# Two-layer hybrid encoder: adds of squares on GpSimd, an earlier root, and border work of the MLP in another order

## The chip, the core and the metric

The kernel runs on one core of a Trainium2 chip. The metric is the device time of one execution in microseconds. Six actors matter: TensorE (PE, with its weight loads PEld), VectorE (DVE), ScalarE (ACT), GpSimd (POOL), SyncE (SP), which issues most loads, and the DMA engines. Each engine works through its own queue in a fixed order.

## The reference

A batch of one with 512 tokens of 1024 features goes through two residual layers and a final RMS norm, in float32. Layer 0 mixes tokens with two groups of attention heads, layer 1 with neighbourhood attention. Behind each stands the part that this change is about:

```
h = h + sq_relu_mlp(rmsnorm(h, norm_ffn[layer]), ffn_w_up[layer], ffn_w_down[layer])

def rmsnorm(x, g):
    y = x * rsqrt(mean(x * x, axis=-1) + EPS)
    return y * g

def sq_relu_mlp(h, w_up, w_down):          # 1024 -> 4096 -> 1024
    u = relu(h @ w_up)
    return (u * u) @ w_down
```

## The kernel before

**Layout.** The residual stream lies transposed in SBUF: `hT` has eight tiles of 128 features by 512 tokens. Every float32 product is made from rounded parts: a weight is split into a high and a low half (`whi` on ACT, L233 or L363; `wlo` on DVE, L223 or L364), an input likewise, and high x high, high x low and low x high are added in PSUM. So one product step is three matmuls of 512 columns (L606 to L608), and each step needs a `wlo` that DVE has made in time.

**A norm at a seam.** The factor of the RMS norm is put in late. For each feature tile k `split_g` makes the two halves of hT times the gain (L612 on ACT, L613 on DVE), and `sumsq_acc` squares the tile on ACT (L620) and adds the square to `acc` (L622). The sum of the first tile is its square itself, so there are seven adds, all on DVE. Then `compact_r` sums over the partitions by matmuls with a column of ones (L627), a root is made by a dozen small DVE operations (L629, L180 to L190), and transposes (L635) and an ACT copy spread it over all partitions as `rb`. There are three such seams: before the MLP of layer 0 (about 240 to 267 us), before the neighbourhood layer (about 579 to 605) and before the MLP of layer 1 (about 804 to 828). In the MLPs the whole root stands in `norm`, called before step 11 (layer 0) or 13 (layer 1) of the 32 steps of the first product `four`. At the neighbourhood seam `rows_r1` stands in the loop over the first value product.

**Seven products instead of eight.** The larger part of both MLP matrices goes through `Seven`: blocks of two by two weight tiles and two token halves, with sums of weight tiles made ahead (`seven_chunk`, L357 to L359) and seven products of 256 columns per pair of input tiles (L450 to L452). The weight sums are on GpSimd; in the four seven-products of the down matrix the fourth pair (kp == 3) has them on DVE. Results are put together on DVE (L459 to L462), and added to hT (L1576).

**The MLP in order.** The up matrix makes 32 tiles: six by plain steps (`plain`), the rest in pairs by seven-products; some of these pairs stay raw (`R`), and in layer 0 one pair more (`V`). The down matrix takes the first six tiles by `product`, the next eight by `product8` (eight banks of PSUM), then the raw pairs by four seven-products m = 0 to 3 (`u7`), and the last pair by plain steps (`gens4`). While `product8` runs, `convert` turns the raw pairs into what `u7` needs: differences on DVE (L391, L394, L423), then rounding on ACT (L418) and the low half on DVE (L419). It is a generator that `mlp` advances by a set pace per step of `product8`; beside it bias rows for the neighbourhood layer are written through SP (L1492, L1497). The plain pair of layer 0 is split (L966 on ACT, L963 on DVE) beside m = 0, after four of its steps.

**What sets the order.** Around attention the order is written out by hand (`fixed_order`). In the MLPs a planner of the framework places each engine's instructions by its own estimate of their times, within the dependences; what is wrapped in `keep_in_program_order` keeps its place. So a source edit at one place can move instructions at others.

Of the kernel before, what the change touches and what calls it, by code (L numbers as in the profile page):

```python
# [35 lines left out]
def encoder_kernel(ctx: ExitStack, tc: tile.TileContext, ins, out, dbg=None):  # L36
    nc = tc.nc
    PE, ACT, DVE, POOL, SP = nc.tensor, nc.scalar, nc.vector, nc.gpsimd, nc.sync
# [37 lines left out]
    def bank(tag, bufs):  # L76
        return ps.tile([P, 512], F32, tag=tag, bufs=bufs, name=nm(tag))

    def mmb():
        return bank("mm", 3)  # L80

    def sbk():
        return bank("s", 2)

    def stb():
        return bank("t", 2)

    def ob():
        return bank("o", 1)

    def scratch(dt=F32):
        return scp.tile([P, 512], dt, tag="sc", name=nm("sc"))
# [177 lines left out]
    def plan(*spec, make=None):  # L270
        asked.append((make or chunk, spec))
        return len(asked) - 1
# [96 lines left out]
    class Seven:  # L369
# [62 lines left out]

        def plan(self, w, c0, pairs=None):

            return [plan(w, pairs[kp] if pairs else 2 * kp, c0, DVE if pairs and kp == 3 else None, make=seven_chunk)
                    for kp in range(self.np)]

        def run(self, ids, evac):
# [130 lines left out]
    def tiles(c0, n):  # L569
        return [(c0 + o, min(P, n - o)) for o in range(0, n, P)]  # L570
# [46 lines left out]
    def sumsq_acc(k, acc, eng=None):  # L617

        sq = acc if k == 0 else scratch()
        ACT.activation(sq, hT[:, k, :], AF.Square)  # L620
        if k:
            (eng or POOL).tensor_tensor(acc, acc, sq, op=ALU.add)  # L622

    def compact_r(acc):
        b = stb()
        for i in range(4):
            PE.matmul(b[:, i : i + 1], acc[:, i * P : (i + 1) * P], ones[:, 0:1], start=True, stop=True)  # L627
        v = tiny(4)
        DVE.tensor_scalar(v, b[:, 0:4], 1.0 / D, EPS, op0=ALU.mult, op1=ALU.add)  # L629
        return rsqrt(v, 4)  # L630
# [8 lines left out]
    acc = pp.tile([P, S], F32, tag="p", name=nm("acc"))  # L639
# [701 lines left out]
    def first_product(l):  # L1341

        w = ins["ffn_w_up"][l]
        X = [Slot() for _ in range(KD)]
        acc = pp.tile([P, S], F32, tag="p", name=nm("acc"))
        for k in range(KD):
            split_g(hT[:, k, :], gffn(l, k), X[k].pair())
            sumsq_acc(k, acc, DVE)
        xp = [s_.pair() for s_ in X]
        U, R = [], []  # L1350
        rb = keep([P, S], F32, "rb")
# [10 lines left out]

        def norm():
            r = compact_r(acc)
            bk = stb()
            bcast_cols(lambda i: r[:, i : i + 1].to_broadcast([P, P]), P, bk)
            ACT.activation(rb, bk, AF.Copy)

        def x_sums(kp):
            raw = Slot(F32)  # L1370
# [39 lines left out]
        def plain():  # L1410
            four = product(w, 0, xp, tiles(0, 512), ev, lambda n: [mmb(), mmb(), mmb(), sbk()])
            two = product(w, 0, xp, tiles(512, 256), ev, lambda n: [sbk(), ob()], kstep=4)
            for n, _ in enumerate(four):
                if n == (11 if l == 0 else 13):
                    norm()
                if n == 14:
                    x_sums(0)
                    x_sums(1)
            for n, _ in enumerate(two):
                if n == 4:  # L1420
                    x_sums(2)
                if n == 6:
                    x_sums(3)
            flip[0] = 1
            for s_ in X:
                s_.free()
            state["plain"] = True
# [74 lines left out]
    def convert(u7, R):  # L1502
        held = tc.keep_in_program_order
        for kp, raw in enumerate(R):
            yield from u7.sums(kp, raw, DVE, held)
            yield
            yield from u7.split(kp, held)

    def mlp(l, last=None):

        stage, ahead, later = first_product(l)
        reserve[0] = 3
        w = ins["ffn_w_down"][l]
        up4, gens4 = [], []

        def plain_last(k0, V):
            left = list(V)  # L1520
            gens4.extend(product(w, k0, up4, tiles(512 * c, 512), lambda j, b, c=c: ev(4 * c + j, b), nk=2 * len(V))
                         for c in range(2))

            def beside(m, i):
                if m == 0 and i % 8 == 4 and left:
                    w_ = left.pop(0)
                    for z in range(2):
                        U4.append(Slot())
                        up4.append(U4[-1].pair())
                        split(w_.t[:, S * z : S * z + S], up4[-1])  # L1530
                    w_.free()

            return beside

        U4 = []

        def ev(m, b):
            return DVE.tensor_tensor(hT[:, m, :], hT[:, m, :], b, op=ALU.add)

        U, _, _, (at_u, _), _ = stage(SIZES[l][0])  # L1540
        up = [s_.pair() for s_ in U]
        gens = [product(w, at_u, up, tiles(512 * c, 512), lambda j, b, c=c: ev(4 * c + j, b)) for c in range(2)]
        ahead()
        for c, gen in enumerate(gens):
            for i, _ in enumerate(gen):
                later(c, i)
        for s_ in U:
            s_.free()
        U, R, V, (at_u, at_r), late = stage(*SIZES[l][1:])
        first = [k + z for k in at_u for z in range(2)]  # L1550
        gen = product8(w, first, U, ev)
        u7 = Seven(2 * len(R))
        ids = [u7.plan(w, 256 * m, at_r) for m in range(4)]
        k0 = 32 - 2 * len(V)
        beside = (last or plain_last)(k0, V)
        bias = iter(()) if last else bias_rows()
        reserve[0] = NSLOT
        work, at = convert(u7, R), 0
        for i, _ in enumerate(gen):
            if i in (1, 4, 6):  # L1560
                next(late, None)
            next(bias, None)

            at += 9 * len(R) + 2
            while at > 0:
                next(work, None)
                at -= 8 * len(U) - 2
        for x in (work, bias):
            for _ in x:
                pass  # L1570
        reserve[0] = 3
        for m in range(4):

            def evac(w_):
                h2 = hT[:, 2 * m : 2 * m + 2, :]
                DVE.tensor_tensor(h2, h2, w_.t.rearrange("p (z n) -> p z n", z=2), op=ALU.add)  # L1576

            for i, _ in enumerate(u7.run(ids[m], evac)):
                beside(m, i)
        u7.free()  # L1580
        if not last:
            hold["tables"].free()
        for gen in gens4:
            for _ in gen:
                pass
        for s_ in U4:
            s_.free()
# [5 lines left out]
    acc = pp.tile([P, S], F32, tag="p", name=nm("acc"))  # L1593
# [227 lines left out]
    for n, _ in enumerate(first):  # L1821
        if n == 2:
            for k in range(KD):
                sumsq_acc(k, acc, DVE)
        if n == 23:
            rows_r1()
    for _ in second:
# [247 lines left out]
```

## Time and profile before

| | us |
|---|---|
| median of 3 runs | 1160.41 (1160.13 to 1161.12) |
| profiled execution | 1159.82 |
| its span, first to last instruction | 1158.0 |
| mean granted TensorE clock | 0.998 |

A row of the timeline gives start and duration in us from the start of the span, engine, line, operation, tiles (written <- read), shape, and in brackets the idle time of the engine just before and what ended it; `x3` merges neighbours of one form. A matmul's duration is its passage through a pipeline, so the distance between two starts, not the duration, tells the rate. In a row of groups stand the busy time, the mean in ns of one, and the idle time before it. A row of a line's view has the shortest, the median and the longest duration in ns.

### The profile page before, as it was taken

How to read it: one execution, taken by the hardware profiler on the slowest of the kernel's cores; microseconds unless marked ns; L12 is line 12 of the kernel's file. 1: busy time of each engine (PE TensorE's matmuls, PEld its weight loads, DVE VectorE, ACT ScalarE, POOL GpSimd, SP SyncE). 2: the span in 40 equal slices, each digit the busy share in tenths (PEclk: the TensorE clock that was granted, in tenths of full speed). 3: DMA queues.
4: the chain of work that ended last, by engine and by line, in shares of the span. 5: the costliest groups of instructions: out<-in, count | busy, mean ns of one | idle time of the engine just before them, and what ended most of it. 6: DMA issues, size and time to landing. Idle time of an engine off the chain costs nothing.

```text
span 1158.0 us, 20534 instructions
## 1 busy us (share of the span) xinstructions
PE 1145.2 (99%) x7348; PEld 1022.7 (88%) x7348; DVE 893.7 (77%) x1568; ACT 669.2 (58%) x1135; POOL 585.3 (51%) x719
## 2 busy tenths in 40 slices
PE   9999999999999999999999999999999999999997
PEld 7787888888899999899988998988889999989995
DVE  7887988878867786977784666667997777688865
ACT  6676877755346668643453555555552666773445
POOL 4356252207688892369602232221388889435840
PEclk9999999999999999999999999999999999999999
DMA  7322415222523237823536574433344223381332
GB/s 236 104 73 72 99 55 137 65 67 96 172 76 98 86 92 192 217 88 110 159 98 164 142 181 119 127 107 119 100 155 127 74 85 99 74 200 58 126 119 73
DMA packets 115350, 134.37 MB, mean 116 GB/s; under 512 B 9795, under 2 KB 96752, under 8 KB 115248
## 3 DMA queue, kind: packets, MB, share of 16 engines
q1 hardware_dynamic: 110896, 120.09, 34.8%
q0 software_dynamic: 4032, 12.60, 5.4%
q8 instruction: 58, 0.95, 0.3%
q14 instruction: 44, 0.36, 0.1%
q10 hardware_dynamic: 320, 0.36, 0.1%
HBM read 110.61 MB, written 6.29 MB: 101 GB/s over the span
## 4 chain that ended last, share of the span: by engine, by line
PE 89%; DVE 5%; DMA 3%; ACT 1%; issue 1%; POOL 0%; SPq 0%; DVEq 0%; POOLq 0%; ACTq 0%
PE mm L606 8%; PE mm L607 8%; PE mm L608 8%; PE mm L452 4%; PE mm L450 4%; PE mm L451 4%; PE s L1130 3%; PE t L450 3%; PE t L452 3%; PE t L451 3%; PE o L1118 3%; PE s L452 2%; PE s L450 2%; PE s L451 2%; PE t L1105 2%; PE s L606 2%
## 5 line engine op out<-in xcount | busy, mean ns | idle before, releaser
L606 PE MATMUL mm<-a,whi 128*128 128x512 f32 x428 | 173.9, 407 | 0.2
L364 DVE TENSOR_TENSOR wlo<-a,whi 128x896 fp32r<-128x896 f32 x103 | 125.4, 1219 | 59.1 <-ACT whi L363 58.6
L608 PE MATMUL mm<-a,wlo 128*128 128x512 f32 x428 | 168.9, 396 | 0.0
L607 PE MATMUL mm<-a,whi 128*128 128x512 f32 x428 | 168.9, 395 | 0.0
L363 ACT ACTIVATE whi<-a 128x896 fp32r<-128x896 f32 x103 | 97.8, 950 | 111.4 <-PE s L451 27.4
L233 ACT ACTIVATE whi<-raw 128x1024 fp32r<-128x1024 f32 (+3 forms) x100 | 92.2, 924 | 68.4 <-PE s L607 24.3
L223 DVE TENSOR_TENSOR wlo<-raw,whi 128x1024 fp32r<-128x1024 f32 (+4 forms) x97 | 110.4, 1143 | 26.9 <-ACT whi L233 26.4
L452 PE MATMUL mm<-a,wlo 128*128 128x256 f32 x430 | 120.6, 280 | 0.4 <-DVE wlo L364 0.4
L450 PE MATMUL mm<-a,whi 128*128 128x256 f32 x430 | 120.8, 281 | 0.0
L451 PE MATMUL mm<-a,whi 128*128 128x256 f32 x430 | 120.5, 280 | 0.0
L363 ACT ACTIVATE whi<-raw 128x896 fp32r<-128x896 f32 x61 | 57.8, 952 | 80.2 <-POOL raw L359 36.1
L358 POOL TENSOR_TENSOR a<-a 128x256 f32<-128x256 f32 x103 | 97.8, 950 | 8.1
L364 DVE TENSOR_TENSOR wlo<-raw,whi 128x896 fp32r<-128x896 f32 x61 | 73.6, 1221 | 35.0 <-ACT whi L363 35.0
L359 POOL TENSOR_TENSOR a<-a 128x128 f32<-128x128 f32 x103 | 95.7, 929 | 8.1
L608 PEld LDWEIGHTS mm<-a,wlo 128*128 128x128 f32 x428 | 80.4, 188 | 18.2
L606 PEld LDWEIGHTS mm<-a,whi 128*128 128x128 f32 x428 | 80.5, 188 | 17.1 <-issue 0.9
L607 PEld LDWEIGHTS mm<-a,whi 128*128 128x128 f32 x428 | 80.7, 189 | 14.9 <-DVE a L963 0.2
L1718 POOL TENSOR_SCALAR p<-p,ti 128x256 f32<-128x256 f32 x64 | 35.8, 570 | 105.7 <-DVE ti L1717 90.7
L1138 POOL TENSOR_SCALAR p<-p,ti 128x512 f32<-128x512 f32 x64 | 45.3, 708 | 85.9 <-DVE ti L1137 59.9
L450 PE MATMUL t<-a,whi 128*128 128x256 f32 x312 | 87.6, 281 | 0.0
L451 PE MATMUL t<-a,whi 128*128 128x256 f32 x312 | 87.4, 280 | 0.0
L452 PE MATMUL t<-a,wlo 128*128 128x256 f32 x312 | 87.4, 280 | 0.0
(432 smaller groups left out, 3574.9 us busy)
## 6 DMA issues: line engine op xcount, KB each, us to landing
a<-in_ffn_w_up_dram SPq DMA_DIRECT2D x102, 256.0 KB, 2.8
raw<-in_ffn_w_down_dram SPq DMA_DIRECT2D x34, 512.0 KB, 4.1
raw<-in_ffn_w_down_dram SPq DMA_DIRECT2D x59, 256.0 KB, 2.7
raw<-in_od_w_qkv_dram SPq DMA_DIRECT2D x64, 128.0 KB, 3.3
raw<-in_ffn_w_up_dram SPq DMA_DIRECT2D x12, 512.0 KB, 3.9
wlo<-in_ffn_w_down_dram POOLq DMA_DIRECT2D x12, 512.0 KB, 7.0
a<-a SPq DMA_DIRECT2D x18, 256.0 KB, 3.2
bx<-a SPq DMA_DIRECT2D x32, 128.0 KB, 5.9
```

The source lines that it names most:

```text
L223: z = lambda: (eng or DVE).tensor_tensor(to, src, f32(high), op=ALU.subtract)
L233: ACT.activation(hi[:, 0:m], raw[:, 0:m], AF.Copy)
L358: held(eng.tensor_tensor(r[:, 4:6], r[:, 2:3].to_broadcast([P, 2, P]), r[:, 0:7:6], op=ALU.add))
L359: held(eng.tensor_tensor(r[:, 7], r[:, 3], r[:, 5], op=ALU.subtract))
L363: ACT.activation(hi[:, 0:896], raw[:, 128:1024], AF.Copy)
L364: DVE.tensor_tensor(lo[:, 0:896], raw[:, 128:1024], f32(hi[:, 0:896]), op=ALU.subtract)
L450: PE.matmul(o, wh, x[:, 0], start=kp == 0 and n in (0, 1, 3, 5), stop=False, skip_group_check=True)
L451: PE.matmul(o, wh, x[:, 1], start=False, stop=False, skip_group_check=True)
L452: PE.matmul(o, wl, x[:, 0], start=False, stop=kp == self.np - 1, skip_group_check=True)
L606: PE.matmul(o, wh, xh, start=first, stop=False)
L607: PE.matmul(o, wh, xl, start=False, stop=False)
L608: PE.matmul(o, wl, xh, start=False, stop=last)
```

## The change

Five edits. (1) At the three seams the adds of tiles 1 to 4 are made by GpSimd, those of tiles 5 to 7 by DVE. (2) `norm` is a generator with two parts, column sums with the root, and the spreading; they are called before steps 8 and 12 of `four` in layer 0, before steps 11 and 14 in layer 1. (3) In the first of the four seven-products of the down matrix (m = 0) the fourth pair's weight sums are on GpSimd too. (4) The plain pair of layer 0 is split beside m = 1. (5) `convert` is advanced by ten steps before `product8` begins, with the same pace afterwards, in both layers.

In the order in which the instructions of the two built programs stand, the following moves on TensorE: column sums (L627) and spreading (L635) stand 9 and 4 instructions earlier at the first seam; 20 and 17 earlier at the second; at the third the sums stand 4 later, because four low products that the planner had put behind them now stand in their places, and the spreading 4 earlier. On DVE one weight split (L223) moves out of the root's chain at the second seam, and one moves into it at the first; one of the plain pair's low halves (L963) moves behind the first evacuation of `u7`. On ACT the conversion's copies (L418) stand further ahead. On SP several loads of the down matrix (L252, L352) stand ahead of bias rows that they followed. Nothing else is added or removed: the matmuls, and the DMAs with their sizes, are the same.

```diff
--- before.py
+++ after.py
@@ -432,7 +432,8 @@
 
         def plan(self, w, c0, pairs=None):
 
-            return [plan(w, pairs[kp] if pairs else 2 * kp, c0, DVE if pairs and kp == 3 else None, make=seven_chunk)
+            return [plan(w, pairs[kp] if pairs else 2 * kp, c0, DVE if pairs and c0 and kp == 3 else None,
+                         make=seven_chunk)
                     for kp in range(self.np)]
 
         def run(self, ids, evac):
@@ -1345,7 +1346,7 @@
         acc = pp.tile([P, S], F32, tag="p", name=nm("acc"))
         for k in range(KD):
             split_g(hT[:, k, :], gffn(l, k), X[k].pair())
-            sumsq_acc(k, acc, DVE)
+            sumsq_acc(k, acc, DVE if k > 4 else POOL)
         xp = [s_.pair() for s_ in X]
         U, R = [], []
         rb = keep([P, S], F32, "rb")
@@ -1362,9 +1363,11 @@
 
         def norm():
             r = compact_r(acc)
+            yield
             bk = stb()
             bcast_cols(lambda i: r[:, i : i + 1].to_broadcast([P, P]), P, bk)
             ACT.activation(rb, bk, AF.Copy)
+            yield
 
         def x_sums(kp):
             raw = Slot(F32)
@@ -1410,9 +1413,10 @@
         def plain():
             four = product(w, 0, xp, tiles(0, 512), ev, lambda n: [mmb(), mmb(), mmb(), sbk()])
             two = product(w, 0, xp, tiles(512, 256), ev, lambda n: [sbk(), ob()], kstep=4)
+            factor = norm()
             for n, _ in enumerate(four):
-                if n == (11 if l == 0 else 13):
-                    norm()
+                if n in ((8, 12), (11, 14))[l]:
+                    next(factor)
                 if n == 14:
                     x_sums(0)
                     x_sums(1)
@@ -1522,7 +1526,7 @@
                          for c in range(2))
 
             def beside(m, i):
-                if m == 0 and i % 8 == 4 and left:
+                if m == 1 and i % 8 == 4 and left:
                     w_ = left.pop(0)
                     for z in range(2):
                         U4.append(Slot())
@@ -1556,6 +1560,8 @@
         bias = iter(()) if last else bias_rows()
         reserve[0] = NSLOT
         work, at = convert(u7, R), 0
+        for _ in range(10):
+            next(work)
         for i, _ in enumerate(gen):
             if i in (1, 4, 6):
                 next(late, None)
@@ -1821,7 +1827,7 @@
     for n, _ in enumerate(first):
         if n == 2:
             for k in range(KD):
-                sumsq_acc(k, acc, DVE)
+                sumsq_acc(k, acc, DVE if k > 4 else POOL)
         if n == 23:
             rows_r1()
     for _ in second:
```

## The prediction

> **What bounds the kernel now.** I read the page's busy shares and chain first, then every start of a matrix product in the timeline, and then the queues that stand behind the few late starts.
>
> ```profile
> PE 1145.2 (99%) x7348; PEld 1022.7 (88%) x7348; DVE 893.7 (77%) x1568; ACT 669.2 (58%) x1135; POOL 585.3 (51%) x719
> PE 89%; DVE 5%; DMA 3%; ACT 1%; issue 1%; POOL 0%; SPq 0%; DVEq 0%; POOLq 0%; ACTq 0%
> ```
>
> TensorE holds the span: it is busy for 1145.2 of 1158.0 us. DVE's 5% of the chain comes from the borders and seams that this change touches. Nothing but a later or an earlier start on TensorE can move the end, so the question is where products start late. A product with 512 columns follows the one before by 0.23 us, one with 256 by 0.12; larger steps are stalls:
>
> ```profile
> 497.12 0.28 PE L451 MATMUL s<-a,whi 128*128 128x256 f32 x1
> 498.62 0.39 PE L452 MATMUL s<-a,wlo 128*128 128x256 f32 x1 [1.22 <-DVE wlo L364]
> ...
> 501.08 0.28 PE L451 MATMUL s<-a,whi 128*128 128x256 f32 x1
> 501.42 0.39 PE L452 MATMUL s<-a,wlo 128*128 128x256 f32 x1
> ...
> 524.22 0.39 PE L452 MATMUL mm<-a,wlo 128*128 128x256 f32 x1 [0.36 <-DVE wlo L364]
> ...
> 592.73 0.28 PE L1674 MATMUL o<-whi,a 128*128 128x256 f32 x1
> 592.85 0.28 PE L1675 MATMUL o<-wlo,a 128*128 128x256 f32 x1
> ...
> 598.88 0.40 PE L608 MATMUL mm<-a,wlo 128*128 128x512 f32 x1
> 599.11 0.40 PE L606 MATMUL mm<-a,whi 128*128 128x512 f32 x1
> 599.66 1.05 PE L627 MATMUL t<-ones,acc 128*128 128x1 f32 x8
> ...
> 604.49 0.65 PE L635 MATMUL t<-cst,r 128*128 128x128 f32 x4 [0.19 <-DVE r L1601]
> ```
>
> Layer 0's border loses 1.50 - 0.12 = 1.38 us at 497, 0.34 - 0.12 = 0.22 at 501 and 0.4 at 524; the seam before the neighbourhood layer loses 0.55 - 0.23 = 0.32 at 599.66 and 0.19 at 604.49. That is 2.5 us in all, so these steps can win little; a new wait in front of TensorE costs in full.
>
> **The change part by part.** First the border of layer 0, where the second weight chunk of the seven products comes late.
>
> ```profile
> 457.93 0.69 DVE L419 TENSOR_TENSOR a<-a,a 128x512 fp32r<-128x512 f32 x1 [1.09 <-ACT a L418]
> 462.89 0.69 DVE L419 TENSOR_TENSOR a<-sc,a 128x512 fp32r<-128x512 f32 x1 [1.81 <-ACT a L418]
> 485.30 0.83 DVE L357 TENSOR_TENSOR raw<-raw 128x128 f32<-128x128 f32 x1 [0.87 <-DMA raw<-in_ffn_w_down_dram]
> 487.25 0.41 DVE L358 TENSOR_TENSOR raw<-raw 128x256 f32<-128x256 f32 x1
> 488.79 0.28 DVE L359 TENSOR_TENSOR raw<-raw 128x128 f32<-128x128 f32 x1
> 494.00 1.17 DVE L419 TENSOR_TENSOR a<-a,a 128x512 fp32r<-128x512 f32 x1
> 495.09 0.68 DVE L1538 TENSOR_TENSOR hT<-hT,o 128x512 f32<-128x512 f32 x1
> 496.28 1.28 DVE L963 TENSOR_TENSOR a<-a,a 128x512 fp32r<-128x512 f32 x2
> 497.49 1.08 DVE L364 TENSOR_TENSOR wlo<-raw,whi 128x896 fp32r<-128x896 f32 x1
> ```
>
> ```profile
> 495.20 0.63 ACT L966 ACTIVATE a<-a 128x512 fp32r<-128x512 f32 x1 [1.65 <-DVE a L419]
> 495.74 2.62 ACT L363 ACTIVATE whi<-raw 128x896 fp32r<-128x896 f32 x3
> ```
>
> ```profile
> 493.19 0.62 POOL L357 TENSOR_TENSOR raw<-raw 128x128 f32<-128x128 f32 x1 [6.41 <-DMA raw<-in_ffn_w_down_dram]
> 493.88 0.73 POOL L358 TENSOR_TENSOR raw<-raw 128x256 f32<-128x256 f32 x1
> 494.70 0.79 POOL L359 TENSOR_TENSOR raw<-raw 128x128 f32<-128x128 f32 x1
> ```
>
> The chunk's low half (L364 at 497.49) is behind the conversion's last operations on DVE, and its high half (L363 at 495.74) is behind L966 on ACT, which waited 1.65 us for the same conversion. Three edits relieve this place. The fourth chunk's sums of the first seven-product leave DVE: 0.83 + 0.41 + 0.28 = 1.5 us; on GpSimd they cost 0.62 + 0.73 + 0.79 = 2.1, hidden by its own idle time (6.41 us before 493.19), but DVE pays some back, since an L419 beside GpSimd took 1.17 for 0.69. I count this edit as 0.2 won. In the built order one of the two low halves of the plain pair (0.6 us) now stands behind the first evacuation; the other stays ahead of this chunk: 0.6 won. The ten steps ahead put ACT's copies in front, so that DVE's waits for them (1.09 and 1.81 us in two rows) shrink: between 0 and 2.9, and I take 1.5, as loads ordered earlier on SP feed the same ACT queue. Together 2.3 us earlier, where 1.4 is needed: both stalls go, **-1.6 us**; ends 0 and -2.0 (with the 0.4 at 524). That later wait I leave: the evacuations on DVE that it follows are unchanged, and the moved split now stands right behind it. SP's loads for the eight-bank product go ahead of bias rows that nobody needs before the neighbourhood layer; if a bias row were late, TensorE would show it at 620. In layer 1 TensorE waits for no low half at the border, so the same edits win nothing; the cover is that the low halves there end before their products, and without it a slip costs its own length: 0, ends 0 and +0.6 (one low half).
>
> Then the adds of squares. What an add on GpSimd costs, and what it does to DVE:
>
> ```profile
> L1373 DVE SCALAR_TENSOR_TENSOR a<-hT,gT,rb x16: 746/1222/1794, 266.7 to 836.1; 128x512 f32<-128x512 f32 x16
> L613 DVE SCALAR_TENSOR_TENSOR a<-hT,gT,a x24: 743/746/751, 242.3 to 818.8; 128x512 fp32r<-128x512 f32 x24
> 272.04 5.22 DVE L1373 SCALAR_TENSOR_TENSOR a<-hT,gT,rb 128x512 f32<-128x512 f32 x4
> 587.82 3.40 DVE L613 SCALAR_TENSOR_TENSOR a<-hT,gT,a 128x512 fp32r<-128x512 f32 x5
> L391 POOL TENSOR_TENSOR a<-a 128x512 f32<-128x512 f32 x8 | 14.1, 1760 | 72.3 <-DVE a L1373 72.3
> L862 POOL TENSOR_TENSOR a<-a 128x512 f32<-128x512 f32 x3 | 3.9, 1294 | 1.1 <-PE s L1130 1.1
> ```
>
> L1373 and L613 are one operation. Alone it takes 746 ns and five take 3.40 us; beside GpSimd's L391 four take 5.22, half the speed. GpSimd's 128x512 operation takes 1294 ns where DVE leaves it alone and 1760 beside DVE. Additions from PSUM are spared: L1538 at 495.09 kept its 0.68 beside L359.
>
> The Trainium skill ("SBUF — State Buffer", Who interferes with whom) says that a DVE instruction with two SBUF inputs and a GpSimd instruction that reads SBUF exclude each other for the whole instruction, while one SBUF input is spared. The rows above agree on which operations suffer; the length is the open point, and its sum is the second rival.
>
> GpSimd has no other work at these seams: what it did last before the seam is long over, and what stands behind the adds in its queue waits for the seam's own results.
>
> *Seam before the neighbourhood layer.*
>
> ```profile
> 584.85 0.61 ACT L620 ACTIVATE sc<-hT 128x512 f32<-128x512 f32 x1
> 591.14 2.35 DVE L223 TENSOR_TENSOR wlo<-raw,whi 128x1024 fp32r<-128x1024 f32 x2
> 595.22 4.38 DVE L622 TENSOR_TENSOR acc<-acc,sc 128x512 f32<-128x512 f32 x6
> ```
>
> The first square is ready at 585.5. Four adds at 1.76 fill GpSimd until 592.5. In these 7.0 us DVE has two PSUM additions (1.2 us) and otherwise L613: 5.8 us at half speed lose 2.9. Four adds at 4.38 / 6 = 0.73 leave DVE: 2.9 won. So the sum is complete at about 599.6, as before. But in the built order the column sums (L627) now stand 20 products earlier, 16 of 0.12 and four of 0.23: 2.8 us of products are queued behind a wait that ends when it did. The first part of it shows earlier: L1675 at 592.85 needs the low half that DVE ended at 592.3 and now ends 2.9 later. The root's chain loses a 1.2 us weight split from its middle, so the 0.19 at 604.49 goes. **+2.6 us**; ends -0.5 (no slowing, both stalls gone) and +3.7 (rival 2).
>
> *Seam before layer 1's MLP.*
>
> ```profile
> 811.26 1.23 DVE L223 TENSOR_TENSOR wlo<-raw,whi 128x1024 fp32r<-128x1024 f32 x1
> 821.56 0.95 PE L627 MATMUL t<-ones,acc 128*128 128x1 f32 x8
> 823.48 0.15 DVE L629 TENSOR_SCALAR ti<-t 128x4 f32<-128x4 f32 x1
> 826.15 0.16 DVE L190 SCALAR_TENSOR_TENSOR ti<-ti,ti 128x4 f32<-128x4 f32 x1
> ```
>
> Three adds at 1.76 from 807.5 (the first square) hold the L223 of 811.26 until 812.8: 1.5 late. From there to 823.48 DVE had no pause; it loses one add, 0.7. The root starts at 823.5 + 1.5 - 0.7 = 824.3 and takes 2.8: 827.1. TensorE has the column sums four products later (822.5) and the broadcast (L635) 12 products behind them (822.5 + 0.8 + 2.8 = 826.1). **+0.9 us**; ends 0 and +1.5.
>
> *Seam before layer 0's MLP.* Column sums stand nine products earlier, the broadcast four. By the same walk the last add still ends ahead of the column sums. A weight split of 1.2 us (L223) now stands inside the root's chain, against five more products of 0.23 between sums and broadcast: 0, ends -0.4 and +0.6 (half a split).
>
> The sum: -1.6 + 2.6 + 0.9 = +1.9 us on the profiled 1159.8. The runs' median, 1160.4, lies 0.6 above the profiled execution, so I forecast **1162.3 us**. What a measurement of this kernel can tell from no change is about 0.2%, 2.3 us; the forecast is within it.
>
> **The rivals.** *1, the border keeps its stall (slower).* If ACT's copies ahead win nothing, the low half of 497.49 comes only 0.2 + 0.6 = 0.8 us sooner and TensorE still waits 0.6. For it: ACT's L966 and L363 stay in the conversion's wake. Against: the two DVE rows with 1.09 and 1.81 us of waiting. It decides when the head start is worth less than 0.6 us. Time: 1162.3 + 0.8 = 1163.1, slower by 0.23%.
>
> *2, the lock in full (slower).* If DVE stands still for the whole of each 1.29 us add, it loses 4 x 1.29 - 1.2 = 4.0 at the neighbourhood seam and not 2.9, and 0.3 more at 811: 1162.3 + 1.4 = 1163.7. That is the result by the rule of the Trainium skill named above. Against: four L1373 beside busy GpSimd lost 5.22 - 2.7 = 2.5, 0.6 each.
>
> *3, the adds find gaps (faster).* If GpSimd's adds slip between DVE's operations, the sum is ready 2.9 us earlier, at 596.7, where the earlier column sums ask for it: -1.6 at the border, -0.4 for the later wait at 524 as DVE gets ahead, -0.5 here and nothing at the other seams: 1160.4 - 2.5 = 1157.9. For it: L1538 is not slowed. Against: L613 has L1373's form.
>
> *4, nothing moves:* the scheduler's order hides all; 1160.4.
>
> **How the numbers follow.** The forecast 0.42, rival 1 0.23, rival 2 0.14, rival 3 0.17, rival 4 0.04. Rivals 1 and 2 lie past 2.3 us, and a little of the forecast's own spread (1160.7 to 1163.2) too, about as much as of theirs lies inside: slower 0.37, faster 0.17, within 0.46. The range goes from rival 3 to rival 2, a little past both ends: 1157.5 to 1164.6.
>
> **What would show it.** Right: no step above 0.3 us among the first forty L450 to L452 of layer 0; L613 over 1 us in the neighbourhood seam; L1675 waiting some 2 us for a low half (L223); L635 of layer 1 waiting for DVE. Wrong: L613 still at 746 ns beside GpSimd's adds, or the 1.2 us wait still on the second chunk. The forecast fails most easily in the length of DVE's slowing, since 2.8 us of products hang on it.

## The result, and the profile after

The changed kernel takes 1163.81 us (median, 1162.71 to 1166.42), the kernel before beside it 1160.74 (1158.91 to 1161.21). The ratio is 1.0031, 95% interval 1.0022 to 1.0040: 3.1 us slower by the medians and 3.6 by the ratio, about 0.3%, where 1162.3 was forecast. The profiled execution took 1163.58 us, 3.8 over that of before.

Busy times and shares of the changed kernel:

```profile
PE 1146.4 (99%) x7348; PEld 1023.2 (88%) x7348; DVE 897.8 (77%) x1550; ACT 668.8 (58%) x1135; POOL 612.1 (53%) x737
```

GpSimd gained 27 us, DVE lost none (897.8 after 893.7): DVE has 18 operations fewer and is busy longer. The changed kernel has a few source lines more, so that L613, L622 and L1675 of the kernel before are L614, L623 and L1681 in it.

To see where the time went I took the distance between the starts of neighbouring products, less 0.232 us for one of 512 columns, 0.118 for one of 256 and the usual distance for the few narrower ones, and summed what is left by stretches of the span. The last column is the same kernel run again, an experiment below.

| stretch, us | before | changed | changed again |
|---|---|---|---|
| 0 to 240 | 10.5 | 11.1 | 10.7 |
| 240 to 290, layer 0's MLP seam | 0.20 | -0.13 | -0.11 |
| 440 to 535, layer 0's border, m = 0 and 1 | 1.69 | -0.46 | -0.33 |
| 535 to 580, m = 2 and 3 | -0.20 | 0.89 | 1.10 |
| 580 to 608, neighbourhood seam | 0.94 | 4.38 | 3.40 |
| 608 to 630, first scores | 0.65 | 1.12 | 1.00 |
| 630 to 800 | 2.57 | 1.72 | 2.03 |
| 800 to 835, layer 1's MLP seam | -0.03 | 0.79 | 0.51 |
| all | 14.9 | 18.7 | 18.0 |

Stretches that the change doesn't touch move by up to 0.6 us from one execution to the next, so terms below that are read only where the step itself is seen in the timeline. The bounds are fixed, and the first profile of the changed kernel is late enough that a step of 0.25 us, which stands ahead of 800 in the other two columns (at 798.62 in the kernel before), falls behind it at 801.18. Counted alike, 630 to 800 is lower by 0.5 to 0.6 in both profiles of the changed kernel, and layer 1's seam higher by 0.5 to 0.6. For the stretch from 630 to 800 I found no reason in the edits; the kernels below read 2.0 to 2.8 there.

**The border** lost its stalls, and a new one stands in m = 2. TensorE's timeline of the changed kernel (start, duration, idle time before in brackets), then DVE's:

```profile
497.29 0.28 PE L452 MATMUL s<-a,whi 128*128 128x256 f32 x1
497.41 0.28 PE L453 MATMUL s<-a,wlo 128*128 128x256 f32 x1
...
541.92 0.28 PE L452 MATMUL s<-a,whi 128*128 128x256 f32 x1
542.97 0.38 PE L453 MATMUL s<-a,wlo 128*128 128x256 f32 x1 [0.78 <-DVE wlo L364]
```

```profile
495.02 1.09 DVE L364 TENSOR_TENSOR wlo<-raw,whi 128x896 fp32r<-128x896 f32 x1 [0.97 <-ACT whi L363]
...
540.16 1.49 DVE L1582 TENSOR_TENSOR hT<-hT,a 128x1024 f32<-128x1024 f32 x1
541.58 2.61 DVE L364 TENSOR_TENSOR wlo<-raw,whi 128x896 fp32r<-128x896 f32 x2
```

The second chunk's low half now ends at 496.1, a microsecond before the chunk's first product, where before it came 1.56 after it. But at 541.92 TensorE waits 0.93 for another low half, behind an evacuation (L1582) on DVE.

**The neighbourhood seam.** TensorE, then DVE, then GpSimd:

```profile
591.76 0.28 PE L1680 MATMUL o<-whi,a 128*128 128x256 f32 x1
594.22 0.38 PE L1681 MATMUL o<-wlo,a 128*128 128x256 f32 x1 [2.18 <-DVE wlo L223]
...
595.35 0.41 PE L1682 MATMUL o<-whi,a 128*128 128x256 f32 x1
595.56 0.41 PE L1680 MATMUL o<-whi,a 128*128 128x256 f32 x1
...
599.50 0.95 PE L628 MATMUL t<-ones,acc 128*128 128x1 f32 x8
```

```profile
585.54 1.04 DVE L614 SCALAR_TENSOR_TENSOR a<-hT,gT,a 128x512 fp32r<-128x512 f32 x1
...
587.10 5.93 DVE L614 SCALAR_TENSOR_TENSOR a<-hT,gT,a 128x512 fp32r<-128x512 f32 x5
592.96 2.35 DVE L223 TENSOR_TENSOR wlo<-raw,whi 128x1024 fp32r<-128x1024 f32 x2
```

```profile
584.64 6.52 POOL L623 TENSOR_TENSOR acc<-acc,sc 128x512 f32<-128x512 f32 x4 [15.47 <-ACT sc L621]
```

Six L614 beside GpSimd's four adds take 1.04 + 5.93 = 6.97 us, where they took 0.75 + 3.40 before: 2.8 lost. So the low half is late, and TensorE waits 2.46 - 0.12 = 2.3 us at 591.76. Behind the wait stands something that the prediction did not have: products 0.21 us apart and not 0.12. Busy time of each engine in short stretches of the changed kernel, in the order PE, PEld, DVE, ACT, POOL (the number behind POOL is the granted TensorE clock, 1.00 for full speed):

```profile
591.47:594.88 3.41, 1.23 (x10) 1.02 (x10) 3.41 (x5) 1.06 (x1) 0.00 (x0) 1.00 0.00 0
...
595.20:598.30 3.10, 3.10 (x16) 3.10 (x16) 3.06 (x5) 0.00 (x0) 0.00 (x0) 0.50 0.45 117
...
598.31:598.70 0.39, 0.39 (x6) 0.39 (x5) 0.06 (x1) 0.00 (x0) 0.00 (x0) 1.00 0.73 212
```

From 594.88 to 598.30, 3.41 us, the clock was at half. In the 3.41 us before that, TensorE had been idle for 2.18.

**Layer 1's seam** shows the wait that was forecast, at half its size: 0.70 - 0.23 = 0.47 us.

```profile
828.24 0.39 PE L608 MATMUL s<-a,whi 128*128 128x512 f32 x1
828.94 0.32 PE L636 MATMUL t<-cst,ti 128*128 128x128 f32 x1 [0.31 <-DVE ti L190]
```

### The profile page after: what moved, and what is told of

Same layout as the page of the kernel before. It is cut to its first block, busy times and chain, and to the rows that moved or that the text cites. A ratio compares the mean times of both kernels' runs of the same rounds, so it can differ in the third digit from the quotient of the medians.

```text
span 1161.8 us, 20533 instructions
## 1 busy us (share of the span) xinstructions
PE 1146.4 (99%) x7348; PEld 1023.2 (88%) x7348; DVE 897.8 (77%) x1550; ACT 668.8 (58%) x1135; POOL 612.1 (53%) x737
## 4 chain that ended last, share of the span: by engine, by line
PE 90%; DVE 4%; DMA 2%; issue 2%; ACT 1%; POOL 1%; SPq 0%; DVEq 0%; ACTq 0%; POOLq 0%
PE mm L607 8%; PE mm L608 8%; PE mm L609 8%; PE mm L453 4%; PE mm L451 4%; PE mm L452 4%; PE s L1131 3%; PE t L451 3%; PE t L453 3%; PE t L452 3%; PE o L1119 3%; PE t L1106 2%; PE s L609 2%; PE s L607 2%; PE s L608 2%; PE s L453 2%
## 5 line engine op out<-in xcount | busy, mean ns | idle before, releaser
L363 ACT ACTIVATE whi<-a 128x896 fp32r<-128x896 f32 x103 | 97.8, 949 | 108.9 <-PE s L452 28.9
L223 DVE TENSOR_TENSOR wlo<-raw,whi 128x1024 fp32r<-128x1024 f32 (+4 forms) x97 | 113.1, 1171 | 28.6 <-ACT whi L233 28.1
L363 ACT ACTIVATE whi<-raw 128x896 fp32r<-128x896 f32 x61 | 57.7, 952 | 83.4 <-POOL raw L359 42.4
L358 POOL TENSOR_TENSOR a<-a 128x256 f32<-128x256 f32 x103 | 94.9, 922 | 8.1
```

The source lines that it names most:

```text
L223: z = lambda: (eng or DVE).tensor_tensor(to, src, f32(high), op=ALU.subtract)
L358: held(eng.tensor_tensor(r[:, 4:6], r[:, 2:3].to_broadcast([P, 2, P]), r[:, 0:7:6], op=ALU.add))
L363: ACT.activation(hi[:, 0:896], raw[:, 128:1024], AF.Copy)
```

## The experiments

Every time is stated against the kernel before, run beside it on the same chip; experiments measured together share those runs.

### 1. The adds of the neighbourhood seam put back on DVE

```diff
# against the changed kernel, at the neighbourhood seam
-                sumsq_acc(k, acc, DVE if k > 4 else POOL)
+                sumsq_acc(k, acc, DVE)
```

> The changed kernel with the seven adds of the neighbourhood seam on DVE again; all else as changed. Theory A (GpSimd's four adds slow DVE, the low half of the second value weights comes late, TensorE waits 2.35 us and then runs some 3 us at half clock): both go, five L614 take 3.4 us again and not 5.93, the excess of 580 to 608 us falls from 4.4 to about 1, and the kernel, 3.1 us slower than before as changed, ends 0.3 below before: 1160.4 us. Rival B (the wait comes from the border work and the loads that were moved, which arrive late at this seam): the wait stays, and the time is within 0.5 us of the changed kernel's 1163.8.

Measured: 1159.78 us against 1159.95, ratio 0.9998 (0.9989 to 1.0007). All 3.1 us are gone. DVE's five operations have their old length:

```profile
587.04 3.40 DVE L614 SCALAR_TENSOR_TENSOR a<-hT,gT,a 128x512 fp32r<-128x512 f32 x5
```

The stretch from 580 to 608 lost 0.89 us, as before; the wait at 542 is still there (0.98), and layer 1's seam waits 0.48. So one of the five edits, at one of the three seams, makes the whole loss, and the other edits together are worth nothing: what the border wins goes elsewhere.

### 2. Those adds alone

```diff
# against the kernel before, at the neighbourhood seam
-                sumsq_acc(k, acc, DVE)
+                sumsq_acc(k, acc, DVE if k > 4 else POOL)
```

> The kernel before with one thing changed: adds 1 to 4 of the neighbourhood seam on GpSimd. Theory A: a wait of about 2.3 us for the low half L223 behind chunk 1's first product, then a stretch of about 3 us at a granted clock of 0.5, together +3.4 us: 1164.1. If the first attention scores' later wait (0.5 us more in the changed kernel) belongs to this seam too, 1164.6. Rival B: no wait, within 0.5 us of before.

Measured: 1163.05 against 1159.95, ratio 1.0025 (1.0015 to 1.0035), 2.9 us slower. TensorE's timeline has the wait; the stretches below it have no half clock:

```profile
593.49 0.28 PE L1674 MATMUL o<-whi,a 128*128 128x256 f32 x1
595.87 0.39 PE L1675 MATMUL o<-wlo,a 128*128 128x256 f32 x1 [2.10 <-DVE wlo L223]
```

```profile
591.52:594.93 3.41, 2.25 (x19) 2.04 (x18) 3.41 (x5) 1.68 (x3) 1.28 (x1) 1.00 0.00 0
594.93:598.35 3.42, 2.48 (x20) 2.49 (x21) 3.42 (x4) 0.00 (x0) 0.00 (x0) 1.00 0.28 78
```

Theory A holds for the wait (2.26) and falls for the clock. The same wait, almost to a tenth, left the clock alone; the seam lost 3.40 - 0.94 = 2.5 us and not 3.4. Something beside the wait's length decides, which experiments 5, 6 and 10 take up.

TensorE meets the last add at 600.07 here and met it at 599.66 before, so the sum is complete about when it was, as the prediction had it. Moving the adds to GpSimd also moves the column sums in the built order, and no run keeps them at their old place. An estimate from these rows: without that move the wait of 2.3 would have covered the 0.3 that TensorE waited at the sums before, and the loss would be about 2.0.

### 3. The border edits alone

```diff
# against the kernel before
-  ... DVE if pairs and kp == 3 else None, make=seven_chunk)
+  ... DVE if pairs and c0 and kp == 3 else None, make=seven_chunk)
-                if m == 0 and i % 8 == 4 and left:
+                if m == 1 and i % 8 == 4 and left:
         work, at = convert(u7, R), 0
+        for _ in range(10):
+            next(work)
```

> The kernel before with the three border edits alone (weight sums of m = 0 on GpSimd, plain pair split beside m = 1, ten steps of the conversion ahead). Theory A: the waits of 1.38, 0.22 and 0.5 us in layer 0's seven-products go (-2.1 us), a new one of 0.8 to 1.0 us for a low half (L364) comes at about 542, in the third seven-product, and layer 1's border costs up to 0.4: 1159.7 us, between 1159.0 and 1160.3. Rival B (the wait at 542 has nothing to do with these edits): 1158.6. Rival C (the waits go only because the earlier root lets the whole MLP start differently): no gain, 1160.7.

Measured: 1159.86 against 1159.95, ratio 0.9998 (0.9989 to 1.0007). The trace has both halves of theory A: 440 to 535 falls from 1.69 to -0.45, and 535 to 580 rises from -0.20 to 0.95. The net of 1 us is at the edge of what the runs can tell, and they show none. Rival B is out, since the wait at 542 is here without any other edit, and rival C too, since the waits at 497 and 501 go without the earlier root. Here TensorE's timeline has it too, and on ACT stands the first sign of where it comes from:

```profile
541.94 0.28 PE L452 MATMUL s<-a,whi 128*128 128x256 f32 x1
543.04 0.38 PE L453 MATMUL s<-a,wlo 128*128 128x256 f32 x1 [0.82 <-DVE wlo L364]
```

```profile
520.95 0.63 ACT L967 ACTIVATE a<-a 128x512 fp32r<-128x512 f32 x1 [2.92 <-DVE hT L1579]
521.49 1.78 ACT L363 ACTIVATE whi<-raw 128x896 fp32r<-128x896 f32 x2
```

The moved pair's high half (L967) waits 2.92 us on ACT for the evacuation of m = 0, with a chunk's high half (L363) queued behind it. On DVE the pair's low half (L964) then stands ahead of that chunk's low half, and a few microseconds later GpSimd waits for a load:

```profile
522.05 0.94 DVE L964 TENSOR_TENSOR a<-a,a 128x512 fp32r<-128x512 f32 x1
522.91 4.16 DVE L364 TENSOR_TENSOR wlo<-raw,whi 128x896 fp32r<-128x896 f32 x3
...
529.00 0.46 POOL L357 TENSOR_TENSOR raw<-raw 128x128 f32<-128x128 f32 x1 [0.79 <-DMA raw<-in_ffn_w_down_dram]
```

Experiment 8 shows what becomes of it.

### 4. Two adds in place of four at the seam

```diff
# against the changed kernel, at the neighbourhood seam
-                sumsq_acc(k, acc, DVE if k > 4 else POOL)
+                sumsq_acc(k, acc, DVE if k > 2 else POOL)
```

> The changed kernel with only adds 1 and 2 of the neighbourhood seam on GpSimd (3 to 7 on DVE). Each add on GpSimd cost DVE 0.72 us of L614 in the changed kernel (2.9 for four). Theory A: with two the low half is 1.45 us earlier, TensorE waits about 0.9 us for it, and as the kernel before had a wait of 1.38 us without any loss of clock, the clock stays at 1.00: 1.4 + 1.5 = 2.9 us faster than the changed kernel, 1160.9. Rival B (the half clock follows any wait at this place): about 1.4 us faster, 1162.4, with a stretch at 0.5. Rival C (DVE's slowing isn't proportional to the adds): the wait stays near 2.3 us.

Measured: 1160.62 against 1159.95, ratio 1.0003 (0.9994 to 1.0012): 0.3 us over before by the ratio, where the changed kernel is 3.2 to 3.6 over by the same measure. GpSimd, DVE and TensorE:

```profile
584.45 3.10 POOL L623 TENSOR_TENSOR acc<-acc,sc 128x512 f32<-128x512 f32 x2 [15.79 <-ACT sc L621]
```

```profile
585.35 1.04 DVE L614 SCALAR_TENSOR_TENSOR a<-hT,gT,a 128x512 fp32r<-128x512 f32 x1
...
586.91 3.84 DVE L614 SCALAR_TENSOR_TENSOR a<-hT,gT,a 128x512 fp32r<-128x512 f32 x5
```

```profile
591.57 0.28 PE L1680 MATMUL o<-whi,a 128*128 128x256 f32 x1
591.95 0.38 PE L1681 MATMUL o<-wlo,a 128*128 128x256 f32 x1
```

The time is theory A's, the working is not. I had divided the loss of four adds by four. Two adds cost DVE (1.04 - 0.75) + (3.84 - 3.40) = 0.73 us, the next two another 2.1. While the first adds run, DVE has additions from PSUM between its L614s, which GpSimd does not disturb (L1542 kept 0.67); the later ones meet nothing but L614. So the wait is 0.26 and not 0.9: the loss is not proportional to the number of adds, though not in the way that rival C had it.

### 5. The changed kernel again

> The changed kernel once more, to see whether the stretch at half clock behind the 2.35 us wait comes again. In the first profile it lasted 3.41 us, and the clock's steps lie on a grid of 3.413 us that starts with the execution. Theory A: the clock is set window by window on that grid, and a window goes to half when the window before it was idle for more than some share between 0.36 (the kernel before: 1.22 of 3.41 us idle, full clock) and 0.64 (2.18 us, half clock); the wait itself is the same in each run, so the stretch comes only when the wait falls mostly into one window. Rival B: every wait of 2 us at this place costs the stretch, and it comes again whatever the grid. Time by both: 3.1 us over before.

Measured: 1163.67 against 1160.05, ratio 1.0028 (1.0018 to 1.0038). The wait is the same 2.34 us; the clock stayed at full. Two stretches, behind the wait and around most of it:

```profile
594.30:597.90 3.60, 3.60 (x30) 3.60 (x31) 3.57 (x5) 0.00 (x0) 0.00 (x0) 1.00 0.53 146
590.31:593.72 3.41, 1.78 (x16) 1.57 (x14) 3.41 (x4) 1.28 (x2) 0.90 (x1) 1.00 0.00 0
```

In the records of the clock, each whole stretch at one clock is a multiple of 3.413 us long: 590.51 us (173 of them) from the first step to full speed to the drop in the first profile. The expectation has the grid start with the execution; it does not, since its first step comes 4.38 us into the span in the first profile and 6.63 in this one. Laid on that grid, the wait here splits into 1.63 us in one window and 0.55 in the next, as in experiment 2 it split into 1.16 and 0.93; in the first profile 2.18 fell into one. Theory A holds, rival B is out. The half clock cost 4.38 - 3.40 = 1.0 us of that profile, not the 1.5 that the products show, since without it TensorE meets the last add: its column sums (L628) come at 598.48, 0.4 after they could.

### 6. Other work inside the wait

```diff
# against the changed kernel, in the loop over the first value product
+        if n == 15:
+            warm = stb()
+            for _ in range(8):
+                PE.matmul(warm[:, 0:P], ones, ones, start=True, stop=True)
         if n == 23:
             rows_r1()
```

> The changed kernel with eight products of ones put ahead of chunk 1 of the values, some 1.8 us of TensorE work into an unused PSUM bank inside the 2.35 us wait (left over: about 0.5 us). Theory A (idle time alone lowers the clock): no row below full clock between 590 and 600, products 0.118 us apart behind the wait; the low half L223 ends when it did. The column sums stand eight products earlier in this build and meet the last add, which ends at about 598.4, so that the time falls by no more than 0.5 us against the changed kernel: +2.6 to +3.1 over before. Rival B (the slow products come from something else, the loads or DVE beside them): products stay 0.21 apart for about 3 us.

Measured: 1162.95 against 1160.05, ratio 1.0027 (1.0017 to 1.0037), within the band. TensorE's timeline, in which the eight products stand as sixteen records:

```profile
591.68 1.95 PE L1834 MATMUL t<-ones 128*128 128x128 f32 x16
...
594.14 0.39 PE L1681 MATMUL o<-wlo,a 128*128 128x256 f32 x1 [0.40 <-DVE wlo L223]
```

The granted clock behind the wait is 1.00 and the products are 0.12 apart, as theory A says; but since experiment 5 has it too, this run by itself does not tell the theories apart. It shows the other half: in this build the column sums stand eight products earlier, and TensorE waits 1.36 us there for the last add, although the clock stayed up. DVE's chain to the last add sets this seam.

### 7 and 8. One border edit undone at a time

Without the head start:

```diff
# against experiment 3
         work, at = convert(u7, R), 0
-        for _ in range(10):
-            next(work)
```

> The kernel before with two of the three border edits: weight sums of m = 0 on GpSimd and the plain pair split beside m = 1, without the ten steps of the conversion ahead. The prediction's steps give the sums 0.2 and the moved low half 0.6, so that the first wait (1.38 at 497) falls to about 0.6 and the head start is worth the rest: 1160.6, 0.6 to 1.0 over the three edits together. Rival B (the head start is worth nothing): both waits are gone here too and the time is that of the three edits, 1159.9. Rival C (the other two are worth nothing): the waits stay at 1.4 and 0.2.

With the plain pair split beside m = 0 as before:

```diff
# against experiment 3
-                if m == 1 and i % 8 == 4 and left:
+                if m == 0 and i % 8 == 4 and left:
```

> The kernel before with two of the three border edits: weight sums of m = 0 on GpSimd and ten steps ahead, the plain pair split beside m = 0 as before. Theory A (the wait of 0.98 at 542 comes from the pair's split in m = 1, whose low halves L964 bunch DVE against GpSimd's weight sums): the wait at 542 is below 0.3, the waits at 497 and 501 stay gone but for 0.3 at most, since the second chunk's low half came 1.07 ahead and only 0.6 of DVE comes back: 1159.0, 1.0 below the kernel before. Rival B (the wait moves: with TensorE 2 us earlier the weight sums are the next thing late, wherever the pair is split): 0.7 to 1.0 at 542 again, 1160.

Measured without the head start: 1160.61 against 1160.05, ratio 1.0004 (0.9995 to 1.0013). With the pair at m = 0: 1158.38, ratio 0.9986 (0.9978 to 0.9995), and in a second measurement 1158.76 against 1160.61, ratio 0.9984 (0.9975 to 0.9992).

> The kernel with two of the three border edits (sums of m = 0 on GpSimd, ten steps ahead) again, beside the combined one: 1.4 to 1.7 below the kernel before if its first measurement (ratio 0.9986) holds; within 0.5 of it if that was a chip's chance.

Without the head start TensorE waits 0.40 - 0.12 = 0.28 at 497, and likewise 0.24 at 500, 0.55 at 523 and 0.92 at 544:

```profile
497.26 0.28 PE L452 MATMUL s<-a,whi 128*128 128x256 f32 x1
497.66 0.38 PE L453 MATMUL s<-a,wlo 128*128 128x256 f32 x1
```

The stretch from 440 to 535 reads 1.1 us more than in experiment 3. In the runs' times the difference is 0.7, within their noise.

The second chunk's low half ends 1.56 us after the chunk's first product starts in the kernel before, 0.46 after it without the head start, 0.83 ahead of it with the pair at m = 0, and 1.07 ahead with all three edits. So the head start is worth 1.5 us of this lead. The pair's move is worth 0.24 at most: in the second measurement's profile, of the same kernel, the lead with the pair at m = 0 is 1.06. The remaining 0.9 to 1.1 is left for the weight sums, by subtraction; no run has them alone. The first wait fell to 0.28 and not to 0.6, and rivals B and C of the first expectation are out.

With the pair at m = 0 the wait at 542 is gone (the same two products start at 542.56 and 542.68, 0.12 apart), and of the one at 524 some 0.3 and 0.2 are left in the two profiles. ACT, then GpSimd:

```profile
519.93 0.96 ACT L363 ACTIVATE whi<-raw 128x896 fp32r<-128x896 f32 x1 [1.51 <-PE s L452]
...
528.38 0.46 POOL L357 TENSOR_TENSOR raw<-raw 128x128 f32<-128x128 f32 x1
```

ACT makes a high half at 519.93, where in experiment 3 it stood behind the pair until 521.49, and no L964 stands ahead of the low half on DVE. A low half's end frees the slot into which a later chunk is loaded. In experiment 3 such a load goes out at 524.56, as the low half that began at 522.91 ends, and lands at 528.87, and GpSimd waits 0.79 us for it; here the load for the same chunk goes out at 524.07 and lands at 526.80, and GpSimd does not wait. From 529.00 on the chunk's weight sums, high half and low half follow each other in experiment 3, so that the low half of the seventeenth chunk comes 0.68 us ahead of the chunk's first product there and 1.93 here. All seven profiles with the pair beside m = 1 have GpSimd's wait, 0.69 to 0.95 us long, and none of the others has it. Why that load takes 4.3 us, where most of these loads take about 2.6, no run shows; here the load after it takes as long (525.62 to 529.98), but GpSimd comes to its chunk only at 530.89. Theory A holds for the place: the pair's move loses 1 us at 542 and wins 0.24 at most at 497, where 0.83 were left over without it. At 542 the low half ends 0.27 us before the product that needs it here, so the wait is just avoided.

### 9. The earlier root alone

```diff
# against the kernel before, with norm() as the generator of the change
+            factor = norm()
...
-                if n == (11 if l == 0 else 13):
-                    norm()
+                if n in ((8, 12), (11, 14))[l]:
+                    next(factor)
```

> The kernel before with the earlier root alone in both MLPs, all adds on DVE. Theory A (the root's place, not the adds, makes the differences at the MLP seams): the wait of 0.39 at 265 goes, and layer 1's spreading (L635) waits 0.47 at about 825. Theory B (the adds make them): with the adds on DVE the sum is late for the earlier column sums, so that layer 0's seam shows a new wait of 0.5 or more in front of L627, and layer 1 has no wait at L635.

One execution: 1160.82 against 1160.61. TensorE's spreading products, at layer 0's seam in the kernel before, then at both MLP seams in this one:

```profile
264.72 0.40 PE L606 MATMUL s<-a,whi 128*128 128x512 f32 x1
265.34 0.65 PE L635 MATMUL t<-cst,ti 128*128 128x128 f32 x4 [0.22 <-DVE ti L190]
```

```profile
264.35 0.40 PE L608 MATMUL mm<-a,wlo 128*128 128x512 f32 x1
264.84 0.65 PE L635 MATMUL t<-cst,ti 128*128 128x128 f32 x4
...
827.53 0.39 PE L608 MATMUL mm<-a,wlo 128*128 128x512 f32 x1
827.76 0.60 PE L635 MATMUL t<-cst,ti 128*128 128x128 f32 x4
```

In layer 0 the wait of 0.39 in front of L635 becomes 0.26; there is no new one in front of the sums. In layer 1 there is no wait at all. So the root's place makes neither difference: with the adds on DVE the one seam stays nearly as it was, and the other has no wait at L635. Theory B is right on layer 1 and wrong on its new wait in layer 0. The 0.33 won at the first seam and the 0.5 lost at the third need the adds on GpSimd; whether the adds alone would bring them, no run shows.

### 10. All seven adds on GpSimd

```diff
# against the kernel before, at the neighbourhood seam
-                sumsq_acc(k, acc, DVE)
+                sumsq_acc(k, acc, POOL)
```

> The kernel before with all seven adds of the neighbourhood seam on GpSimd (four gave a wait of 2.3 us, two of 0.26, none of 0). Theory A (DVE loses 1.05 us per add while it makes L613 alone, and the low half's own two-input operation L223 suffers too; GpSimd's chain of seven adds at 1.6 ends at about 597): the wait for L223 grows to 3 to 4 us, and, since more than 0.64 of a window of 3.41 us is then idle in nearly any position, a stretch of one window at half clock follows; 1163.5 to 1165.5. Rival B (only the adds beside L613 count, and the last L613 is done by then): the wait stays at 2.3 us, and with 2.2 us less DVE work behind it the sum is ready sooner: 1162.

Measured: 1167.97 against 1160.61, ratio 1.0061 (1.0046 to 1.0076), 7.1 us slower and more than either theory gave. GpSimd, DVE, TensorE and the stretches behind the wait:

```profile
585.63 11.54 POOL L622 TENSOR_TENSOR acc<-acc,sc 128x512 f32<-128x512 f32 x7 [15.79 <-ACT sc L620]
```

```profile
588.09 7.96 DVE L613 SCALAR_TENSOR_TENSOR a<-hT,gT,a 128x512 fp32r<-128x512 f32 x5
```

```profile
592.81 0.28 PE L1674 MATMUL o<-whi,a 128*128 128x256 f32 x1
598.31 0.58 PE L1675 MATMUL o<-wlo,a 128*128 128x256 f32 x1 [5.21 <-DVE wlo L223]
```

```profile
593.44:596.85 3.41, 0.00 (x0) 0.00 (x0) 3.41 (x3) 0.63 (x1) 3.25 (x3) 1.00 0.00 0
596.85:600.26 3.41, 1.95 (x9) 1.96 (x10) 3.41 (x3) 0.00 (x0) 0.32 (x1) 0.50 0.20 58
600.26:603.68 3.42, 3.42 (x19) 3.42 (x18) 0.26 (x1) 0.00 (x0) 0.00 (x0) 0.50 0.67 180
```

The wait is 5.4 us: 2.3 for four adds and about 1.05 for each of three more, which is theory A's own price; the 3 to 4 in its text came from adding too little. After a window without a single product the clock was at half for two windows, not one. Rival B is out.

### 11. What won, put together

Experiment 8 (pair at m = 0) with the adds of tiles 1 to 4 on GpSimd and the root before steps 8 and 12 in layer 0's seam alone:

```diff
# against experiment 8, with norm() as the generator of the change
-            sumsq_acc(k, acc, DVE)
+            sumsq_acc(k, acc, DVE if l or k > 4 else POOL)
...
-                if n == (11 if l == 0 else 13):
-                    norm()
+                if n in ((8, 12), (13,))[l]:
+                    next(factor)
+                if n == 13 and l:
+                    next(factor)
```

> The kernel before with the parts of the change that won in a trace: weight sums of m = 0 on GpSimd, ten steps ahead, adds 1 to 4 on GpSimd and the earlier root in layer 0's MLP seam alone; plain pair beside m = 0, neighbourhood seam and layer 1's seam as before. Theory A (the parts add up): the border's gain of 1.7 us over the kernel before, and 0.33 more at 240 to 290 us, where the wait of 0.39 at 265 goes: 2.0 below before, ratio 0.998. Rival B (the first seam's gain is given back within layer 0's MLP, since the border there is bounded by DVE and GpSimd): 1.6 below before, as the same kernel without the seam.

Measured: 1158.28 against 1160.61, ratio 0.9980 (0.9971 to 0.9989): 2.3 us faster than the kernel before. It beats both kernels. The same kernel without the seam had 1158.76 beside it; half a microsecond is too little to say that the seam adds its 0.33, though the trace shows it (240 to 290: -0.11 for 0.20).

## Why the prediction was right, and where it was not

The forecast of 1162.3 is 1.5 us below the measured 1163.8, inside the range; the direction is right, and the largest term stands where it was put. The change itself was forecast at 1.9 us, too little to be told from nothing, and measured at 3.1 to 3.6, which is clear of the noise. Term by term, by the first profile and by the kernel run again:

- **Neighbourhood seam, +2.6.** Measured 4.38 - 0.94 = +3.4 and 3.40 - 0.94 = +2.5, and +2.5 with the adds alone. The reason is the one given: L613 at nearly half speed (2.8 us lost for the forecast 2.9), DVE as busy as before, TensorE held first at L1675 for a low half. What the step put off to the column sums shows almost wholly at that first wait, 2.3 us, and 0.4 at the sums where the clock stays up. The price of the slowing was read beside GpSimd's L391 alone, but in that stretch (272 to 277 us of the kernel before) GpSimd ran L394 and L397 as well; it fitted the adds all the same. The half clock, +1.0 where it came, was in no term.
- **Border of layer 0, -1.6.** Measured -2.15 and -2.0: the head start was worth 1.5 as taken, the pair's move 0.24 at most and not 0.6, and 0.9 to 1.1 is left for the weight sums, taken as 0.2. The later wait at 524 (0.52 by the distance of the starts), which the step left as it was, went too.
- **What is late next.** This is the step that failed. It looked at the wait at 524 alone and found the moved pair harmless there. The pair stands in ACT's queue ahead of a chunk's high half and waits for an evacuation, it stands on DVE ahead of that chunk's low half, a load that waits for this low half's slot goes out later, GpSimd waits for the load, and twenty microseconds after the pair a low half is 0.9 to 1.1 late. That is +1.1 and +1.3 of TensorE, in no term, and it eats over half of the border's gain. The forecast counted what the pair left, and not whom it stands in front of at its new place, on ACT and on DVE.
- **Layer 1's MLP seam, +0.9.** Measured +0.5 to +0.6 in both; the wait for the root is there (0.47), half as long as the 1.0 of the step.
- **Layer 0's MLP seam, 0.** -0.33, within its ends (-0.4).
- **Layer 1's border, 0.** The stretch from 1070 on reads 0.3 and 0.5, where the kernel before reads -0.25, but kernels with the same edits read -0.13 and 0.26 there, and one without them 0.40. No verdict; it is scatter of that size.
- **First scores.** Their wait for a DMA (of `a` from a scratch tile, no bias row) is 1.04 and 0.91 us long in the two profiles of the changed kernel and 0.55 in the kernel before. In the other kernels it is between 0 and 0.7, with the moved loads (0.43 in experiment 3) as without them (0.71 in experiment 2), so those loads do not make it. What does stays open.

Rival 1 did not occur: no step above 0.3 us among the first forty products of the border. Rival 2 gave 1163.7, nearest of all to the result, by a price that the runs do not show at four adds: DVE lost 2.8 there, not 4.0. The rule it came from, the Trainium skill ("SBUF — State Buffer", Who interferes with whom), names rightly who suffers. Its whole-instruction lock, with the 1.29 us that a GpSimd operation of this form takes where DVE leaves it alone, would cost DVE as much for each add; where adds met L613 alone the measured price was about 1.05, and beside additions from PSUM 0.37. Rival 3 is out: L613 took over 1 us. That the time came out near the forecast is partly luck, since a missed loss of 1.1 and a missed half clock stood against a border gain that was 0.5 larger, and 0.33 at the first seam.

## What to carry to other kernels

An operation moved to GpSimd is no relief for DVE if both read SBUF with two inputs at that time: here each add saved DVE 0.73 us and cost it up to 1.05, and it came earlier in DVE's queue than what it saved. Before a piece of work is moved, ask on every queue that it enters (here ACT's and DVE's) what it will stand in front of and what it waits for there; undoing that one move of three turned nothing into 1.7 us. Where a stall is taken away, look at all later places with little to spare, not at the next one alone.

## What the runs showed of the hardware

A wait can cost more than itself, by chance. In all profiles here the granted clock changed only on a grid of 3.413 us, and it fell to half in the window behind one in which TensorE was idle for 2.18 us of it (0.64); it did not fall behind windows with 1.63 (0.48), 1.22 (0.36, in the kernel before) or 1.16 us. So the same wait of 2.3 us brought the half clock in one execution and not in two others, depending on how it lay on the grid. After a window with no product at all the clock stayed at half for a second window, though TensorE was busy for 1.95 us of the first. The Trainium skill ("TensorE: Matmul & The Clock Gate", Part 1: The HAM clock gate) has the free-running window of 3413 ns, and the trace agrees (3.41 us). The working rule of the Trainium skill (same page, HAM oscillation — how this bites in real kernels), no idle gap above some 3.4 us, is too mild for what these runs show: 2.2 us was enough.
